# Attention heads issued in pairs over the two halves of the array, with the first mixer's masks added on VectorE

## Chip, core and metric

The kernel runs on one core of a Trainium2 chip. The metric is device time in microseconds for one execution. TensorE multiplies, VectorE and ScalarE work on tiles, SyncE issues the loads of weights. Each engine takes its instructions in the order of its own queue and waits on semaphores for the others.

## The reference

256 tokens of 1024 features go through two blocks. The parts that this change touches are the products of attention heads, all 64 wide:

```python
SEQ, D_MODEL, HEAD_DIM = 256, 1024, 64
ATTN_PATTERNS = ((128, 1), (512, 4), (2048, 16))     # window, dilation of three groups of four heads

def token_mixing(u, cos, sin, w_in, w_pool, pool_scale, w_pool_branch, w_attn_branch, w_out):
    p, q, k, v, gate_logits = jnp.split(u @ w_in, cuts, axis=-1)
    y_pool = multiscale_pool(p, w_pool, pool_scale)            # 4 groups of 64
    q, k = apply_rope(q, cos, sin), apply_rope(k, cos, sin)
    for gi, (window, dilation) in enumerate(ATTN_PATTERNS):
        o, lse = dilated_window_attention(q[:, :, hs], k[:, :, hs], v[:, :, hs], window // dilation, dilation)
    wts = jax.nn.softmax(jnp.stack(lses, axis=0), axis=0)      # joint over the three groups
    y_attn = jnp.einsum('gbsh,gbshd->bshd', wts, jnp.stack(outs, axis=0))
    gates = jax.nn.sigmoid(gate_logits)
    return (g_pool * (y_pool @ w_pool_branch) + g_attn * (y_attn @ w_attn_branch)) @ w_out

def second_block(x, ...):
    for l in range(2):
        ret_o = retention(rq, rk, r_v, r_g, ret_gn_w[l])                       # 4 heads, 64 wide
        swa_o = sliding_window_sink_attention(s_q, s_k, s_v, swa_sinks[l])     # 6 heads, 64 wide
        mla_o = latent_attention(...)                                          # 6 heads, keys of 96, values of 64
        mix = jnp.concatenate([ret_o, swa_o, mla_o], axis=-1) @ w_out[l]
        x = layer_norm(DEEPNORM_ALPHA * x + mix, ...)
        x = layer_norm(DEEPNORM_ALPHA * x + grouped_moe(x, ...), ...)
```

Block 1 is a feed-forward step, this `token_mixing`, and a second feed-forward step, each with its modulation.

## The kernel before

Activations lie transposed, features on partitions and the 256 tokens in the columns. Weights come from HBM as fp32 panels of 1 MB (`raw`, five buffers) and are split exactly into two parts: ScalarE casts the high one and VectorE subtracts it for the low one (both L254, 128x1024 a piece, into `hl`, six buffers). A product with a split weight is `mm3`, three matmuls (L249 to L251). Only the weights' products are split; the products inside attention are plain fp32, which TensorE runs in two pieces, so that a row of the trace counts each of them twice.

A scheduler sets the order on each engine when the program is built. It follows the program's dependences and its own model, and so it mixes a head's products with the split products of a projection. After that each queue is fixed.

The first mixer (`mixer`, L704) projects queries, keys and values, does the pooling branch (`dd`, L761 and L762: two products for each of four groups, two groups in the two column halves of a bank), and then runs a loop of four. An iteration takes the scores of one head in three groups (`scores`, L780 to L783), starts two gate panels, lets three panels of the modulation through (`drain`, each a pass of VectorE at L354 over 128x1024), takes the softmax (`softmax_rows`, L693 to L700), multiplies the gate panels (96 split products, `proj_t`), and then takes the head's values (`values`, L795 to L801). In a group the late 128 queries see 256 keys and the early ones 128. For each a matmul of an identity with the bf16 mask opens the PSUM region, and the 64-row product of queries and keys adds to it. For the values, three transposes go into one bank of the tag `x` (two buffers), `evac` copies 384 columns out as `pt` (two buffers; every third call of `evac` goes to VectorE at L687, the others to ScalarE at L685), and two 64-column products add into `y`.

Block 2 has two layers (`mixer2`). Heads come in pairs there: `pair_scores` (L981) puts the scores of two heads into one PSUM tile, one head after the other, `pair_softmax` normalises them and `pair_values` (L995) transposes, copies and multiplies head by head. The sliding-window pairs have 64 rows and a mask over both key blocks; the latent pairs have 96 rows and a mask over the diagonal block. The retention loop (L1204) takes a head's scores (`rs`, L1210 and L1211), multiplies them with the decay on VectorE (`sd`, L1213) and makes two products into `ry` (L1214, L1215). Other products of these layers are the latent projections, `uq` and `ukv` (L674 to L676), whose banks are copied out by `evac` as well.

PSUM has eight banks: two for `mm`, one each for `st` and `w` (where `y` and `ry` lie), two of the tag `x`, and the tile `s1` of two banks.

## Time and profile before

| | |
|---|---|
| runs | 1182.67, 1182.7, 1187.75 us |
| median of the runs | 1182.7 us |
| span of the profiled execution | 1186.2 us |
| TensorE busy | 1144.6 us, 96% |
| VectorE busy | 713.3 us, 60% |
| ScalarE busy | 511.4 us, 43% |
| DMA, share of 16 engines | 62.8%, 229 GB/s |
| mean granted clock of TensorE | 0.987 |

The profiled execution is one of its own, some 3.5 us longer than the median run. Spans on an engine are busy times of its instructions; a matmul's busy time reaches into the start of the next, so lengths of work on TensorE are best read from start to start.

### The profile page before, as it was taken

How to read it: one execution, taken by the hardware profiler on the slowest of the kernel's cores; microseconds unless marked ns; L12 is line 12 of the kernel's file. 1: busy time of each engine (PE TensorE's matmuls, PEld its weight loads, DVE VectorE, ACT ScalarE, POOL GpSimd, SP SyncE). 2: the span in 40 equal slices, each digit the busy share in tenths (PEclk: the TensorE clock that was granted, in tenths of full speed). 3: DMA queues.
4: the chain of work that ended last, by engine and by line, in shares of the span. 5: the costliest groups of instructions: out<-in, count | busy, mean ns of one | idle time of the engine just before them, and what ended most of it. 6: DMA issues, size and time to landing. Idle time of an engine off the chain costs nothing. (4 is left out here: it accounts for less than half of the span.)

```text
span 1186.2 us, 20785 instructions
## 1 busy us (share of the span) xinstructions
PE 1144.6 (96%) x8495; PEld 943.5 (80%) x8495; DVE 713.3 (60%) x1410; ACT 511.4 (43%) x946; POOL 44.5 (4%) x53
## 2 busy tenths in 40 slices
PE   6999999999999999999999998999989999899995
PEld 4999999988888999999997878544458787844443
DVE  5698879777877775555677754621258864451114
ACT  4454445534534554444556434222247643322213
POOL 0000001000000200000120001000001000100000
PEclk9999999999999999999999999999989999999998
DMA  9788779738863455535572439599743334779941
GB/s 317 292 362 307 288 258 325 263 133 316 306 230 112 173 180 182 184 125 183 168 250 99 143 109 353 216 385 390 290 155 135 136 109 170 288 272 397 380 156 38
DMA packets 77354, 272.12 MB, mean 229 GB/s; under 512 B 7873, under 2 KB 10817, under 8 KB 62914
## 3 DMA queue, kind: packets, MB, share of 16 engines
q1 hardware_dynamic: 77250, 270.70, 62.8%
q8 instruction: 70, 1.15, 0.4%
q14 instruction: 34, 0.28, 0.1%
HBM read 269.63 MB, written 1.05 MB: 228 GB/s over the span
## 5 line engine op out<-in xcount | busy, mean ns | idle before, releaser
L254 DVE TENSOR_TENSOR hl<-raw,hl 128x1024 fp32r<-128x1024 f32 (+5 forms) x267 | 293.4, 1108 | 120.8 <-ACT hl L254 120.0
L254 ACT CAST hl<-raw 128x1024 fp32r<-128x1024 f32 (+5 forms) x267 | 254.0, 958 | 233.9 <-PE mm L251 172.2
L249 PE MATMUL mm<-xh,hl 128*128 128x256 f32 x896 | 255.2, 286 | 4.0 <-ACT xh L254 3.3
L251 PE MATMUL mm<-xh,hl 128*128 128x256 f32 x896 | 255.2, 285 | 0.0
L250 PE MATMUL mm<-xl,hl 128*128 128x256 f32 x896 | 253.4, 283 | 0.0
L249 PEld LDWEIGHTS mm<-xh,hl 128*128 128x128 f32 x896 | 169.6, 190 | 6.6 <-ACT xh L254 3.6
L250 PEld LDWEIGHTS mm<-xl,hl 128*128 128x128 f32 x896 | 170.4, 190 | 1.9 <-issue 1.9
L251 PEld LDWEIGHTS mm<-xh,hl 128*128 128x128 f32 x896 | 170.4, 190 | 1.0 <-issue 1.0
L1632 PE MATMUL gu<-hl,xg 128*64 128x512 f32 x208 | 101.8, 604 | 0.0
L249 PE MATMUL mm<-gh,hl 128*128 128x256 f32 x352 | 99.2, 282 | 0.0
L251 PE MATMUL mm<-gh,hl 128*128 128x256 f32 x352 | 99.2, 282 | 0.0
L250 PE MATMUL mm<-gl,hl 128*128 128x256 f32 x352 | 99.2, 282 | 0.0
L1632 PE MATMUL gu<-raw,xg 128*64 128x512 f32 x192 | 92.9, 603 | 0.0
L354 DVE SCALAR_TENSOR_TENSOR raw<-raw,cond 128x1024 f32<-128x1024 f32 x64 | 76.7, 1219 | 10.0 <-DMA raw<-in_w_ada_dram 10.0
L1668 DVE SCALAR_TENSOR_TENSOR ysl<-dn,gsl,ysh 128x512 fp32r<-128x512 f32 x32 | 23.9, 750 | 75.8 <-ACT ysh L1667 75.8
L250 PEld LDWEIGHTS mm<-gl,hl 128*128 128x128 f32 x352 | 67.0, 190 | 0.0
L249 PEld LDWEIGHTS mm<-gh,hl 128*128 128x128 f32 x352 | 67.0, 190 | 0.0
L251 PEld LDWEIGHTS mm<-gh,hl 128*128 128x128 f32 x352 | 67.0, 190 | 0.0
L1632 PE MATMUL gu<-rawe,xg 128*64 128x512 f32 x112 | 54.6, 604 | 0.0
L1619 DVE TENSOR_SCALAR xg<-ga,cols 128x256 f32<-128x256 f32 x32 | 17.4, 543 | 55.8 <-ACT xg L1618 55.8
L1667 ACT ACTIVATE ysh<-dn,gsl 128x512 fp32r<-128x512 f32 x32 | 22.0, 687 | 55.7 <-PE dn L1665 55.7
L1618 ACT ACTIVATE xg<-ga,cols 128x256 f32<-128x256 f32 x32 | 18.1, 565 | 60.9 <-PE ga L1615 55.0
(531 smaller groups left out, 2428.3 us busy)
## 6 DMA issues: line engine op xcount, KB each, us to landing
raw<-in_w_ffn_in_dram SPq DMA_DIRECT2D x41, 1024.0 KB, 4.9
raw<-in_w_ada_dram SPq DMA_DIRECT2D x34, 1024.0 KB, 6.2
raw<-in_w_in_dram SPq DMA_DIRECT2D x34, 1024.0 KB, 5.0
hl<-in_gate_up_dram SPq DMA_DIRECT2D x26, 1024.0 KB, 8.5
raw<-in_gate_up_dram SPq DMA_DIRECT2D x24, 1024.0 KB, 7.9
raw<-in_w_ffn_out_dram SPq DMA_DIRECT2D x32, 704.0 KB, 4.2
rawe<-in_gate_up_dram SPq DMA_DIRECT2D x14, 1024.0 KB, 8.2
raw<-in_w_out_dram SPq DMA_DIRECT2D x12, 1024.0 KB, 4.9
```

The lines of the kernel that those rows point to most:

```text
L249: PE.matmul(o, wh, xh, start=first, stop=False)
L250: PE.matmul(o, wh, xl, start=False, stop=False)
L251: PE.matmul(o, wl, xh, start=False, stop=last)
L254: return S.copy(hi, x), V.tensor_tensor(out=lo, in0=x, in1=hi.bitcast(F32), op=ALU.subtract)
L354: V.scalar_tensor_tensor(out=w, in0=w, scalar=1.0, in1=cond, op0=ALU.mult, op1=ALU.mult, accum_out=mod[:, a + j:a + j + 1])
L1618: S.activation(out=xg[:, 2 * j], in_=p[:, :T], func=AF.Identity, scale=col(0, 2 * j), bias=col(8, 2 * j))
L1619: mark[0] = V.tensor_scalar(out=xg[:, 2 * j + 1], in0=p[:, T:], scalar1=col(0, 2 * j + 1), scalar2=col(8, 2 * j + 1), op0=ALU.mult, op1=AL ...
L1632: mm = PE.matmul(p[i * CAP:(i + 1) * CAP], xg[:, k, s], w[i][:, k % 4], start=(k == 0), stop=(k == KB - 1))
L1667: made = S.activation(out=ysh[:, c], in_=p, func=AF.Copy, scale=gc)
L1668: mark[0] = made, V.scalar_tensor_tensor(out=ysl[:, c], in0=p, scalar=gc, in1=ysh[:, c].bitcast(F32), op0=ALU.mult, op1=ALU.subtract)
```

## The change

In the first mixer the four heads become two pairs. The masks are no longer products: a pair's scores of a group go into one `s1` tile, a bank to each head, and VectorE adds the mask on the way into an SBUF tile `sb`. The softmax then works inside `sb`. The values of a pair take six transposes into one tile of the same tag `s1` (one buffer), one copy of 768 columns, and four products, the heads in turn. Scores and softmax of a pair stand a gate iteration ahead of the next pair's, and the values one and two iterations later.

```diff
+                def scores(j):
+                    sb = pool.tile([P, 2, 3, 3 * P], F32, name="sb", tag="sb", bufs=2)
                     for g in range(3):
-                        q, k = qT[r, g, h // 2], kT[r, g, h // 2]
-                        PE.matmul(s1[:, g], identb, mask[:, g * T:g * T + T], start=True, stop=False)
-                        PE.matmul(s1[:, g], q[:, P:], k, start=False, stop=True)
-                        PE.matmul(s0[:, g], identb, mask[:, g * T + P:g * T + T], start=True, stop=False)
-                        PE.matmul(s0[:, g], q[:, :P], k[:, :P], start=False, stop=True)
+                        s = pq.tile([P, 2, 2 * T], F32, name="s1", tag="s1", bufs=1)
+                        for i, r in enumerate(halves):
+                            PE.matmul(s[:, i, :T], qT[r, g, j, P:], kT[r, g, j], start=True, stop=True)
+                        for i, r in enumerate(halves):
+                            PE.matmul(s[:, i, T:T + P], qT[r, g, j, :P], kT[r, g, j, :P], start=True, stop=True)
+                        V.tensor_tensor(out=sb[:, :, g], in0=s[:, :, :3 * P], in1=mask[:, g:g + 1].to_broadcast([P, 2, 3 * P]), op=ALU.add)
...
+                def soft(sb):
+                    parts = [sb[:, :, :, :T], sb[:, :, :, T:]]
+                    for x in range(2):
+                        V.tensor_reduce(out=mx[:, 2 * x:2 * x + 2], in_=parts[x], op=ALU.max, axis=AX.XY)
+                    V.tensor_scalar(out=nb, in0=mx, scalar1=-0.125, scalar2=None, op0=ALU.mult)
+                    for p, c in every:
+                        S.activation(out=p, in_=p, func=AF.Exp, bias=nb[:, c], scale=0.125, accum_out=den[:, c])
+                    V.reciprocal(out=den, in_=den)
+                    for p, c in every:
+                        V.tensor_scalar(out=p, in0=p, scalar1=den[:, c], scalar2=None, op0=ALU.mult)
...
+                def values(j, sb):
                     y = bank("w", "y")
                     for g in range(3):
-                        tr = bank("x", "tr", pq)
...
-                        pt = pool.tile([P, 3 * P], F32, name="pt", tag="pt", bufs=2)
-                        evac(pt, tr[:, :3 * P])
-                        PE.matmul(y[r, :T], v[:, g, 0, c], pt[:, :T], start=(g == 0), stop=False)
-                        PE.matmul(y[r, P:T], v[:, g, 1, c], pt[:, T:], start=False, stop=(g == 2))
+                        tr = pq.tile([P, 2, 2 * T], F32, name="tr", tag="s1", bufs=1)
...
+                        pt = pool.tile([P, 2, 3 * P], F32, name="pt", tag="pt", bufs=1)
+                        evac(pt, tr[:, :, :3 * P])
+                        for t, o in enumerate((slice(0, T), slice(P, T))):
+                            for i, r in enumerate(halves):
+                                PE.matmul(y[r, o], v[:, g, t, (2 * j + i) * 64:(2 * j + i) * 64 + 64], pt[:, i, (0, T)[t]:(T, 3 * P)[t]],
+                                          start=(g + t == 0), stop=(g == 2 and t == 1))
...
+                sb = [scores(0)]
+                soft(sb[0])
+                gate(0)
+                sb.append(scores(1))
+                soft(sb[1])
+                gate(1)
+                values(0, sb[0])
+                gate(2)
+                values(1, sb[1])
+                gate(3)
```

`gate(i)` is the rest of the old loop's body. The pooling's products are issued group by group in turn instead of both of one group first. In block 2, the pairs of 64 rows get one mask product of 384 columns a head, and then the two late and the two early products in turn; the latent pairs stay as they were. `pair_values` and the retention go the same way as the first mixer's values: one tile of the tag `s1`, one pass of 768 columns, products in turn.

```diff
+            if q[0].shape[0] == 64:
+                for i in two:
+                    PE.matmul(s[:, 2 * i:2 * i + 2].rearrange("p a t -> p (a t)")[:, :3 * P], identb, mask, start=True, stop=False)
+                for i in two:
+                    PE.matmul(late[i], q[i][:, P:], k[i], start=False, stop=False)
+                for i in two:
+                    PE.matmul(early[i], q[i][:, :P], k[i][:, :P], start=False, stop=True)
...
-                        st = bank("x", "rs", pq)
...
-                        sd = pool.tile([P, 384], F32, name="sd", tag="pt", bufs=2)
-                        V.tensor_tensor(out=sd, in0=st[:, :384], in1=decay[:, 2 * b + i], op=ALU.mult)
...
+                    st = pq.tile([P, 2, 2 * T], F32, name="rs", tag="s1", bufs=1)
...
+                    sd = pool.tile([P, 2, 384], F32, name="sd", tag="pt", bufs=1)
+                    V.tensor_tensor(out=sd, in0=st[:, :, :384], in1=decay[:, 2 * b:2 * b + 2], op=ALU.mult)
```

Comments and docstrings are dropped too, so line numbers differ. The loads on SyncE and the work of GpSimd keep their order, and outside the mixers so does TensorE.

On TensorE in the first mixer, around a group's values: `tr` is the tile of transposes, `y` the values' products, `s` a head's scores (the numbers tell tiles apart). Before:

```order
L795 MATMUL tr<-k_c_mats,pr_3352 128x128
L796 MATMUL tr<-k_c_mats,pr_3361 128x128
L797 MATMUL tr<-k_c_mats,pr_3361 128x128
L780 LDWEIGHTS identb
L780 MATMUL s_3492<-mask,identb 128x256
L781 MATMUL s_3492<-kT,qT 128x256
L800 MATMUL y<-pt,v 64x256
L801 MATMUL y<-pt,v 64x128
L800 MATMUL y<-pt,v 64x256
L801 MATMUL y<-pt,v 64x128
L795 MATMUL tr<-k_c_mats,pr_3352 128x128
L796 MATMUL tr<-k_c_mats,pr_3361 128x128
```

After, with four more split products where the dots are:

```order
L802 MATMUL y<-pt,v 64x256 x2
L802 MATMUL y<-pt,v 64x128 x2
L797 MATMUL tr<-k_c_mats,sb 128x128 x6
L250 MATMUL mm<-xl,hl 128x256
L251 MATMUL mm<-xh,hl 128x256
L249 MATMUL mm<-xh,hl 128x256
...
L251 MATMUL mm<-xh,hl 128x256
L802 MATMUL y<-pt,v 64x256 x2
L802 MATMUL y<-pt,v 64x128 x2
L797 MATMUL tr<-k_c_mats,sb 128x128 x6
```

Before, the products of one head stood between transposes and scores of others; after, eight split products stand between a set of six transposes and the four products that need its copy.

On TensorE in block 2, layer 0, the scores of the third sliding-window pair. Before:

```order
L986 LDWEIGHTS identb
L986 MATMUL s_7218<-mask,identb 128x256
L987 MATMUL s_7218<-skT,sqT 128x256
L991 LDWEIGHTS identb
L991 MATMUL s_7218<-mask,identb 128x128
L992 MATMUL s_7218<-skT,sqT 128x128
L986 LDWEIGHTS identb
L986 MATMUL s_7218<-mask,identb 128x256
L987 MATMUL s_7218<-skT,sqT 128x256
L1000 MATMUL tr<-k_c_mats,pr 128x128
L1001 MATMUL tr<-k_c_mats,pr 128x128
L1002 MATMUL tr<-k_c_mats,pr 128x128
```

After, from the last transposes ahead of the second pair's values on:

```order
L676 MATMUL uq<-hl,cTh_7057 128x288
L1104 MATMUL tr<-k_c_mats,ckv 128x128 x2
L1023 MATMUL y<-pt,sv 64x256 x2
L1023 MATMUL y<-pt,sv 64x128 x2
L998 LDWEIGHTS identb
L998 MATMUL s_7126<-mask,identb 128x384
L998 LDWEIGHTS identb
L998 MATMUL s_7126<-mask,identb 128x384
L1000 MATMUL s_7126<-skT,sqT 128x256 x2
L1002 MATMUL s_7126<-skT,sqT 128x128 x2
L1104 MATMUL tr<-k_c_mats,ckv 128x128 x2
L674 MATMUL ukv<-hl,cTh_7209 128x384
```

The masks went ahead of all products, the two heads' products stand together, and the second pair's values (`y`) stand right ahead of them, where they stood behind.

On VectorE in the first mixer, at the start of the gate loop: `hl` are weight splits, L354 the modulation's panels, `ds` and `ypl` the pooling's. Before:

```order
L254 TENSOR_TENSOR hl<-raw,hl 128x1024 x2
L354 SCALAR_TENSOR_TENSOR raw,mods<-raw,cond 128x1024
L768 SCALAR_TENSOR_TENSOR ypl<-yp,k_pool_scale,yph 128x256
L687 COPY ds<-dd 128x256
L354 SCALAR_TENSOR_TENSOR raw,mods<-raw,cond 128x1024
L768 SCALAR_TENSOR_TENSOR ypl<-yp,k_pool_scale,yph 128x256
L693 TENSOR_REDUCE mx<-s_3303 128x1
L693 TENSOR_REDUCE mx<-s_3302 128x1
L695 TENSOR_SCALAR nb<-mx 128x1
L356 TENSOR_TENSOR mods<-mods,k_b_ada 128x2
L695 TENSOR_SCALAR nb<-mx 128x1
L354 SCALAR_TENSOR_TENSOR raw,mods<-raw,cond 128x1024
```

After:

```order
L254 TENSOR_TENSOR hl<-raw,hl 128x1024 x2
L773 TENSOR_TENSOR sb<-s_3304,mask 128x2x384
L756 SCALAR_TENSOR_TENSOR ypl<-yp,k_pool_scale,yph 128x256
L687 COPY ds<-dd 128x256
L354 SCALAR_TENSOR_TENSOR raw,mods<-raw,cond 128x1024 x2
L756 SCALAR_TENSOR_TENSOR ypl<-yp,k_pool_scale,yph 128x256
L773 TENSOR_TENSOR sb<-s_3310,mask 128x2x384
L356 TENSOR_TENSOR mods<-mods,k_b_ada 128x2
L354 SCALAR_TENSOR_TENSOR raw,mods<-raw,cond 128x1024
L254 TENSOR_TENSOR hl<-raw,hl 128x1024
L773 TENSOR_TENSOR sb<-s_3316,mask 128x2x384
L354 SCALAR_TENSOR_TENSOR raw,mods<-raw,cond 128x1024
```

The two reductions of the first head's scores are gone from here, and three additions `sb` stand among the splits and panels; the reductions follow after the third.

## Rows read from the trace of the kernel before

**Rows 1.** The page, parts 1 and 2: busy us, share, instructions; granted clock in 40 slices
```profile
PE 1144.6 (96%) x8495; PEld 943.5 (80%) x8495; DVE 713.3 (60%) x1410; ACT 511.4 (43%) x946; POOL 44.5 (4%) x53
PEclk9999999999999999999999999999989999999998
```

**Rows 2.** TensorE's waits: waiter, releaser, total us, times, longest
```profile
PE ukv L674 <- DVE vm L687: 1.6, 2, 0.8
```

**Rows 3.** Windows of the gate loop: busy us by engine, granted clock, DMA share, GB/s
```profile
285.60:305.00 19.40, 19.40 (x143) 16.19 (x142) 16.35 (x31) 9.76 (x16) 0.00 (x0) 1.00 0.88 326
305.00:324.00 19.00, 19.00 (x136) 16.17 (x135) 17.04 (x36) 7.73 (x14) 0.00 (x0) 1.00 0.81 307
324.00:343.00 19.00, 19.00 (x134) 15.79 (x133) 13.67 (x30) 7.47 (x14) 0.00 (x0) 1.00 0.65 229
343.00:360.00 17.00, 17.00 (x120) 14.09 (x119) 8.78 (x16) 7.50 (x13) 0.00 (x0) 1.00 0.50 200
```

**Rows 4.** Timeline of TensorE, one head's group: start, us, products (two pieces each in fp32)
```profile
327.55 0.28 PE L780 MATMUL s<-mask,identb 128*128 128x256 bf16 x1
327.76 0.70 PE L781 MATMUL s<-kT,qT 64*128 64x256 f32 x2
...
328.96 0.28 PE L780 MATMUL s<-mask,identb 128*128 128x256 bf16 x1
...
329.80 0.65 PE L800 MATMUL y<-pt,v 128*64 128x256 f32 x2
330.60 0.23 PE L782 MATMUL s<-mask,identb 128*128 128x128 bf16 x1
```

**Rows 5.** Windows, TensorE's products into y alone: layers 0 and 1 of block 2
```profile
600.00:760.00 160.00, 8.31 (x48) 0.99 0.51 182
860.00:1040.00 180.00, 8.79 (x48) 0.97 0.46 164
```

**Rows 6.** Timeline of TensorE: the pooling's products; a retention pair's scores
```profile
287.34 0.66 PE L761 MATMUL dd<-raw,pn 128*64 128x256 f32 x4
287.82 0.40 PE L762 MATMUL dd<-raw,pn 128*64 128x128 f32 x4
288.15 0.28 PE L780 MATMUL s<-mask,identb 128*128 128x256 bf16 x1
...
686.79 0.71 PE L1210 MATMUL rs<-rqT,rkT 64*128 64x256 f32 x4
687.33 0.40 PE L1211 MATMUL rs<-rqT,rkT 64*128 64x128 f32 x4
687.65 0.38 PE L249 MATMUL mm<-mixh,hl 128*128 128x256 f32 x1
687.88 0.28 PE L250 MATMUL mm<-mixl,hl 128*128 128x256 f32 x1
688.00 0.28 PE L251 MATMUL mm<-mixh,hl 128*128 128x256 f32 x1
```

**Rows 7.** Timeline of TensorE: a sliding-window pair's scores, first and following product
```profile
613.08 0.28 PE L986 MATMUL s<-mask,identb 128*128 128x256 bf16 x1
...
615.91 0.38 PE L1025 MATMUL mm<-hl,xh 128*128 128x256 f32 x1
```

**Rows 8.** Windows, the retention's products into ry alone: layer 0
```profile
600.00:760.00 160.00, 2.60 (x16) 0.99 0.51 182
```

**Rows 9.** VectorE by form (xcount, busy us, mean ns, idle before); the first two in 285:367
```profile
L254 DVE TENSOR_TENSOR hl<-raw,hl 128x1024 fp32r<-128x1024 f32 x18 | 22.0, 1221 | 6.7 <-ACT hl L254 6.7
L354 DVE SCALAR_TENSOR_TENSOR raw<-raw,cond 128x1024 f32<-128x1024 f32 x18 | 21.8, 1217 | 0.3 <-DMA raw<-in_w_ada_dram 0.3
...
L687 DVE COPY pt<-tr 128x384 f32<-128x384 f32 x14 | 7.8, 555 | 6.5 <-PE tr L797 3.6 <-PE tr L1002 2.9
L1213 DVE TENSOR_TENSOR sd<-rs,raw 128x384 f32<-128x384 f32 x8 | 4.3, 553 | 2.4 <-PE rs L1211 2.4
```

**Rows 10.** ScalarE by form, whole span: the copy of a head's transposed weights
```profile
L685 ACT COPY pt<-tr 128x384 f32<-128x384 f32 x22 | 10.1, 481 | 9.0 <-PE tr L1002 9.0
```

More of the change, by code (lines that the diff above doesn't have):

```diff
@@ L772, in mixer @@
                 yal = pool.tile([P, 2, T], F32R, name="yal")
-                def scores(h):
-                    r = slice(h % 2 * 64, h % 2 * 64 + 64)
-                    s1 = pq.tile([P, 4, T], F32, name="s1", tag="s1", bufs=1)
-                    s0 = bank("x", "s0", pq).rearrange("p (g k) -> p g k", g=4)
+                halves = [slice(i * 64, i * 64 + 64) for i in range(2)]
+                def scores(j):
+                    sb = pool.tile([P, 2, 3, 3 * P], F32, name="sb", tag="sb", bufs=2)
@@ L800, in values @@
-                        PE.matmul(y[r, :T], v[:, g, 0, c], pt[:, :T], start=(g == 0), stop=False)
-                        PE.matmul(y[r, P:T], v[:, g, 1, c], pt[:, T:], start=False, stop=(g == 2))
-                    split(yah[r, h // 2], yal[r, h // 2], y[r, :T])
+                        tr = pq.tile([P, 2, 2 * T], F32, name="tr", tag="s1", bufs=1)
+                        for i in range(2):
+                            for x, c in enumerate((slice(T, None), slice(0, P), slice(P, T))):
+                                PE.transpose(tr[:, i, x * P:(x + 1) * P], sb[:, i, g, c], ident)
@@ L804, in mixer, with gate @@
+                    split(yah[:, j], yal[:, j], y[:, :T])
                 tg = pool.tile([P, KB, 2 * T], F32, name="tg")
-                for i in range(4):
-                    s0, s1 = scores(i)
+                def gate(i):
                     wgp = weights(win[10 + i], KB, 256)
@@ L982, in pair_scores @@
             s = pq.tile([P, 4, T], F32, name="s1", tag="s1", bufs=1)
-            for i in range(2):
-                o, e = s[:, 2 * i], s[:, 2 * i + 1, :P]
-                if mask.shape[-1] == T:
-                    PE.matmul(o, identb, mask, start=True, stop=False)
-                    PE.matmul(o, q[i][:, P:], k[i], start=False, stop=True)
-                else:
-                    PE.matmul(o, q[i][:, P:], k[i], start=True, stop=False)
-                    PE.matmul(o[:, P:], identb, mask, start=False, stop=True)
-                PE.matmul(e, identb, mask[:, -P:], start=True, stop=False)
-                PE.matmul(e, q[i][:, :P], k[i][:, :P], start=False, stop=True)
+            two = range(2)
+            late, early = [s[:, 2 * i] for i in two], [s[:, 2 * i + 1, :P] for i in two]
+            if q[0].shape[0] == 64:
[5 more added lines that the diff above has]
+                    PE.matmul(early[i], q[i][:, :P], k[i][:, :P], start=False, stop=True)
+            else:
+                for i in two:
+                    PE.matmul(late[i], q[i][:, P:], k[i], start=True, stop=False)
+                    PE.matmul(late[i][:, P:], identb, mask[:, P:T], start=False, stop=True)
+                    PE.matmul(early[i], identb, mask[:, P:T], start=True, stop=False)
+                    PE.matmul(early[i], q[i][:, :P], k[i][:, :P], start=False, stop=True)
             return s
@@ L1045, in mixer2 @@
                 maskf = raw_tile(A["c_masks"].rearrange("p (a m) -> p a m", a=1), 1, 8 * P)[:, :8 * P]
-                mask = pool.tile([P, 2 * P], BF16, name="mask")
-                V.tensor_copy(mask, maskf[:, 6 * P:])
+                mask = pool.tile([P, 3 * P], BF16, name="mask")
+                V.tensor_copy(mask[:, :T], maskf[:, 6 * P:])
+                V.tensor_copy(mask[:, T:], maskf[:, 7 * P:])
                 sk = pool.tile([P, 3, 2, 2], F32, name="sk")
```

77 lines of the change are left out of this document (31 added, 46 removed).

## The prediction, made before the changed kernel ran

> **What bounds the kernel now.** I read the page's busy shares first, then TensorE's list of waits, then windows over the first mixer's attention, and only then single products. TensorE is busy 1144.6 of the 1186.2 us of the span, at the full clock (2.4 GHz, granted clock near 1.00) nearly throughout; VectorE is busy 60% [rows 1]. TensorE idles some 42 us in all. In the gate loop of the first mixer it is busy in every microsecond, VectorE for 16.35 of 19.40 us in the first stretch and 8.78 of 17 in the last, and the DMA share falls from 0.88 to 0.50 [rows 3]. So every product here is on the path: what is taken off TensorE is time saved, if no wait takes its place. The waits that exist are short; the one that resembles what the change adds (a product waiting for a bank that VectorE has yet to copy out) cost 0.8 us at the longest [rows 2].
>
> **Units.** A full 128x256 product of the split weights takes 0.12 us from start to start, and the first one after a plain fp32 product 0.23, so a switch costs 0.11 (687.65, 687.88, 688.00) [rows 6].
>
> **First mixer's scores.** One head and group now takes 1.41 us from its late mask to the next one's (327.55 to 328.96), of which the late mask product alone is 0.21 [rows 4]. There are 12, so 16.9 us. After, a pair of heads has two 256-key and two 128-key products on opposite row halves and no mask. The price of that set is already in the trace: the retention's products have the same shapes, and both heads of a pair ran in 0.86 us (686.79 to 687.65) [rows 6]. Six sets are 5.2 us: 11.7 saved.
>
> **First mixer's values.** The two 64-column products of a head alone take 0.80 us (329.80 to 330.60) [rows 4]; twelve of them are 9.6. The pooling's four products have the same shapes on the two column halves and ran in 0.81 us together (287.34 to 288.15) [rows 6]; six such sets are 4.9. The difference is 4.7; I take 4.5, since a few already stand next to another head's. The 36 transposes stay. The sets stand more often alone between split products, some six more switches at 0.11, 0.6 lost. First mixer: 11.7 + 4.5 - 0.6 = 15.6 us off TensorE.
>
> **Pooling.** Issued in turn now, but both halves overlapped already [rows 6]: nothing. Here the Trainium skill says otherwise. In "TensorE: Matmul & The Clock Gate", Part 3, it states that matmuls keep program order in start and end and are never reordered. By that, four products issued head by head would have run in two serial steps before, and the change would gain some 0.8 us here at each of two places and about as much at the retention, and the time would be 3 us lower than I say; the rows show both heads' first products ahead of either second one, so the trace disagrees and I count nothing.
>
> **Block 2 scores.** One pair of sliding-window heads takes 2.83 us (613.08 to 615.91) [rows 7]; two layers have three each. After: two 384-column mask products, at 0.21 each by the nearest row (the 256-column mask), and a row-half set at 0.86: 1.28. Six times 1.55 is 9.3 saved. The latent pairs have 96 rows and cannot pair: nothing.
>
> **Block 2 values.** 12 pairs held TensorE 8.31 + 8.79 = 17.1 us with tails [rows 5]. One set in turn is 0.88 with its tail (the pooling's, 287.34 to 287.82 and 0.40) [rows 6]: 12 x 0.88 = 10.6. Saved 6.5; some pairs overlap already, which is why it is not half.
>
> **Retention.** The value products of four pairs held 2.60 us in a layer, 1.30 a pair [rows 8]; in turn 0.88, four pairs save 1.7. The score products overlapped where nothing stood between them [rows 6]; for the others I take 0.8. Together 2.5.
>
> Off TensorE in all: 15.6 + 9.3 + 6.5 + 2.5 = **33.9 us**.
>
> **What the change adds.** Six mask additions of 128x768 on VectorE. A 384-wide product read from PSUM takes 553 ns there, a copy 555 [rows 9]; I take 0.95 us for 768. The softmax now reduces from SBUF the same number of elements, two reductions for a pair instead of four, so VectorE gains about 2 us of work against 18.6 us of idle time in the four stretches of the loop [rows 3]: no new bound. DMA and its order are untouched. The costs are hand-offs, because the scores tile and the tile of six transposes are now one PSUM tile with one buffer, and the copy out is one instruction of 768 where two of 384 took turns:
>
> - Scores of groups two and three wait until VectorE has added the mask of the group before. The additions stand in the queue behind two 1.22 us weight splits or modulation panels [rows 9]; queued behind the addition are the pooling's second subtraction, the panels and splits; TensorE stands meanwhile with all the gate products behind it. Walking the queues by the row durations gives 0.3 + 0.85 + 0.6 us for the three places where products ahead do not cover it, bounds 0 and 1.2 us (one split) for each of four.
> - Values: between a set of transposes and its products stand 8 split products at the shortest (0.95 us) and 12 at the longest. The copy of 768 takes 0.85 on ScalarE by twice 481 ns less the fixed part [rows 10], and 0.95 on VectorE plus its queue. Four on ScalarE wait 0.2 to 0.3, the two on VectorE 0.7 and 1.0 behind splits. Together with the scores about **5 us**, bounds 2 and 9.
> - Twelve copies out of PSUM become six, so whose turn it is (every third copy is VectorE's) shifts for all later ones; a 384-wide copy costs 481 or 555 ns by engine [rows 9, 10], so I take no net cost.
> - Block 2, a layer: six copies 0.3 us longer than before, with little cover (1.8); the retention's one multiplication of 768 instead of two of 384 (0.35); and two further waits like the one on a bank at 0.8 [rows 2], since the sliding-window scores and products now come earlier than ScalarE and VectorE deliver (1.6). About 3.75 a layer, **7.5 us**, bounds 3 and 13. Nearest row is the 0.8, so I stay near it.
>
> Net: 33.9 - 12.5 = 21.4 us. The profiled execution has a span of 1186.2, the runs a median of 1182.7; the work removed is the same in both. 1186.2 - 21.4 is 1164.8 for a profile, 1182.7 - 21.4 = 1161.3 for the median: **1161**. With waits between 5 and 22 us the forecast's own range is 1154 to 1171.
>
> **Rivals.**
> 1. *Hand-offs cost twice as much or a little more.* For it: one buffer where there were two, and additions in an in-order queue with 1.2 us pieces ahead. Against: VectorE is free for 16%, 10%, 28% and 48% of the loop's four stretches [rows 3], and the rows show no wait over 0.8 us on such a copy. Waits of 25 us instead of 12.5 leave 9: 1174. The Trainium skill, "TensorEngine Tiling (Array Packing)", section PSUM Bottleneck, says that tiling speeds up TensorE but not the copy out of PSUM, which may then be the bottleneck; that speaks for this rival, and the trace of before, with its double buffers, cannot settle it.
> 2. *Nearly all hidden.* The scheduler's products in between cover the hand-offs but for 2 us: 1151.
> 3. *Slower: the additions fall behind VectorE's queue.* If each of the eight VectorE hand-offs of the first mixer (six additions, two copies) meets two panels of 1.22 us and a split that itself waits for ScalarE (VectorE waited 6.7 us for ScalarE in this loop [rows 9]), 3.6 us each, that is 29 us over the forecast: 1190. It decides from 2.7 us each on. For it: the queue is in order and the addition stands behind exactly such pieces. Against: with a tenth to a half of each stretch idle on VectorE, the queue is seldom three deep.
> 4. *The halves do not overlap in the new order* and the change only drops masks: 12 x 0.21 of the late masks, the early ones at no more than that, so 4.4 with 0.16 for an early one, and 2 in block 2, against 12.5 of waits: 1189. Against: rows 6, the same shapes.
>
> **How the numbers follow.** Forecast 0.58, rival one 0.20, two 0.08, three 0.08, four 0.06. The predicted time is the forecast's. The range of 8 in 10: below 1150 lies a share of rival two, above 1176 rivals three and four and the tail of rival one; 1150 to 1176. A measurement of this kernel tells a difference from no change at about 0.5%, 5.9 us, so from 1177 to 1189. Faster by more holds the forecast, rival two and three quarters of rival one, 0.81; within it a quarter of rival one and a part of three and four, 0.10; slower 0.09.
>
> **What would show it.** In the profile after: the four 64-row products of a pair within about 0.86 us and the four 64-column ones within 0.81 where no wait stands ahead; TensorE's busy time about 30 us lower; its waits 10 to 15 us higher, on the mask addition, on the copies of 768 and, in block 2, on the latent product's bank; VectorE's busy time some 2 us changed, DMA unchanged. The gain should lie about 10 us in the first mixer and 11 us in the two mixers of block 2. I am wrong if single waits on the mask addition reach 2 us, if a half-array set takes 1.4 us or more, or if what is saved comes back as a wait for weights after the loop: the DMA share of 0.88 in the first stretch [rows 3] leaves little to hurry, and panels used up to 10 us earlier may not be there.

## The result, and the profile after

The changed kernel takes 1156.4 us (median of 1155.7 to 1161.73) against 1182.68 us, a ratio of 0.9766 (95% interval 0.9742 to 0.9791): 26.3 us less, where 21.4 were forecast. In a second set of runs the ratio was 0.9782 (0.9759 to 0.9805).

TensorE is still busy 96% of the span, with 34 us less work. The profile's page after has this line, which answers to [rows 1] (busy time, share, instructions):

```profile
PE 1110.8 (96%) x8459; PEld 925.6 (80%) x8459; DVE 715.0 (62%) x1391; ACT 507.9 (44%) x932; POOL 44.5 (4%) x53
```

VectorE gained 1.7 us and the DMA traffic is the same, 272.12 MB. The two profiled spans differ by 31.5 us, more than the medians: before's profiled execution had a start that was 4.2 us longer (221.0 us instead of 216.8 to the first product `la` of the mixer), in code that is the same in both. Its clock was at the low level there, from 28 us on; the window from 28 to 35 us (length, TensorE's busy time, granted clock, DMA share, GB/s), before and after:

```profile
28.00:35.00 7.00, 6.61 (x37) 0.51 1.05 403
...
28.00:35.00 7.00, 7.00 (x62) 1.00 1.05 404
```

This is an accident of the execution: over the 14 profiles of this document, the seven with such a stretch need 219.7 to 221.6 us to that product and the seven without it 216.5 to 217.4, and the changed kernel is in both groups. So I compare stages, cut at the same products in both programs, and not spans.

Four stages, as windows of TensorE: stretch, its length, TensorE's busy time (x instructions), granted clock, DMA share, GB/s. First the kernel before, in this order: the first mixer from its last rotation (`perm`) to the second feed-forward step's first product; layer 0 from its first product to the last router product; the entry of layer 1, from the last expert product to the first into `s`; and layer 1 from there.

```profile
263.85:403.00 139.15, 137.11 (x1031) 1.00 0.64 232
594.55:729.51 134.96, 132.76 (x988) 1.00 0.51 177
875.60:884.98 9.38, 4.58 (x43) 0.81 0.38 102
884.98:1021.88 136.90, 134.02 (x980) 0.99 0.47 167
```

The kernel after, the same four (behind TensorE's busy time stand four more: weight loads, VectorE, ScalarE and GpSimd):

```profile
259.62:383.25 123.63, 122.36 (x1007) 114.88 (x1006) 110.78 (x178) 63.06 (x97) 5.62 (x6) 1.00 0.71 261
574.78:704.14 129.36, 124.88 (x981) 111.93 (x980) 86.42 (x196) 61.84 (x146) 9.68 (x10) 0.99 0.52 185
850.20:862.63 12.43, 4.74 (x42) 3.10 (x41) 4.95 (x17) 5.75 (x16) 0.87 (x1) 0.74 0.51 157
862.63:992.11 129.48, 125.73 (x974) 113.32 (x973) 87.17 (x205) 65.90 (x157) 7.93 (x9) 0.97 0.47 170
```

The first mixer is 15.5 us shorter, the layers 5.6 and 7.4, and the entry of layer 1, whose work is the same, 3.1 us longer. In the first mixer TensorE's idle time (length less busy) did not grow but shrank, from 2.0 to 1.3 us.

Other executions of the changed kernel and of variants show how steady the stages are. The first mixer was 123.6 us in three of three profiles of the changed kernel and 139.2 in two of two of the kernel before. A layer at the full clock was 127.8 us, and 1.6 to 3.1 more where the granted clock fell (below).

The units came as forecast. TensorE's timeline after, a row set of the first mixer, a column set, and a sliding-window pair with its two masks ahead:

```profile
290.33 0.70 PE L770 MATMUL s<-kT,qT 64*128 64x256 f32 x4
290.86 0.39 PE L772 MATMUL s<-kT,qT 64*128 64x128 f32 x4
291.18 0.38 PE L250 MATMUL mm<-xl,hl 128*128 128x256 f32 x1
...
320.29 0.87 PE L802 MATMUL y<-pt,v 128*64 128x256 f32 x8
321.09 0.88 PE L797 MATMUL tr<-k_c_mats,sb 128*128 128x128 f32 x6
...
593.33 0.50 PE L998 MATMUL s<-mask,identb 128*128 128x384 bf16 x2
593.75 0.70 PE L1000 MATMUL s<-skT,sqT 64*128 64x256 f32 x4
594.29 0.39 PE L1002 MATMUL s<-skT,sqT 64*128 64x128 f32 x4
594.61 0.38 PE L1041 MATMUL mm<-hl,xh 128*128 128x256 f32 x1
```

Start to start these are 0.85, 0.80 and 1.28 us, against 2 x 1.41, 2 x 0.80 and 2.83 before [rows 4, 7]. VectorE and ScalarE by form have the prices of the long pieces, 950 to 955 ns and 796 ns, where 0.95 and 0.85 were taken:

```profile
L687 DVE COPY pt<-tr 128x768 f32<-128x768 f32 x8 | 7.6, 955 | 2.8 <-PE tr L1018 2.4 <-PE tr L797 0.4
L773 DVE TENSOR_TENSOR sb<-s,mask 128x768 f32<-128x768 f32 x6 | 5.7, 950 | 0.0
L685 ACT COPY pt<-tr 128x768 f32<-128x768 f32 x10 | 8.0, 796 | 3.7 <-PE tr L1018 1.9 <-PE tr L797 1.8
```

TensorE's waits after (waiter, releaser, total, times, longest), the main ones that are new or longer than before:

```profile
PE ukv L674 <- ACT vm L685: 3.5, 2, 1.7
PE la L251 <- issue: 2.9, 1, 2.9
PE rrb L1253 <- DVE r L1248: 2.6, 2, 1.3
PE tr L1104 <- DVE cq L1096: 1.3, 2, 1.0
PE uq L674 <- ACT qf L685: 0.6, 2, 0.3
PE s L770 <- DVE sb L773: 0.5, 1, 0.5
PE y L802 <- DVE pt L687: 0.2, 1, 0.2
```

None of the hand-offs that the prediction priced is large: 0.5 us for one mask addition and 0.2 for one copy in the first mixer. One wait is nearly gone there: the branch products waited 2.0 us for `e` before (three times) and 0.4 after. The last values now stand ahead of a whole gate iteration, which may be why; no run isolates it.

### The profile page after: what moved, and what is told of

It is laid out like the page before. It is cut to its first block, busy times and chain, and to the rows that moved or that the text cites. A ratio compares the mean times of both kernels' runs of the same rounds, so it can differ in the third digit from the quotient of the medians.

```text
span 1154.7 us, 20672 instructions
## 1 busy us (share of the span) xinstructions
PE 1110.8 (96%) x8459; PEld 925.6 (80%) x8459; DVE 715.0 (62%) x1391; ACT 507.9 (44%) x932; POOL 44.5 (4%) x53
## 2 busy tenths in 40 slices
DMA packets 77354, 272.12 MB, mean 236 GB/s; under 512 B 7873, under 2 KB 10817, under 8 KB 62914
## 5 line engine op out<-in xcount | busy, mean ns | idle before, releaser
L251 PE MATMUL mm<-xh,hl 128*128 128x256 f32 x896 | 254.4, 284 | 0.0
L250 PE MATMUL mm<-xl,hl 128*128 128x256 f32 x896 | 253.3, 283 | 0.0
L250 PEld LDWEIGHTS mm<-xl,hl 128*128 128x128 f32 x896 | 169.6, 189 | 1.8 <-issue 1.6
L251 PEld LDWEIGHTS mm<-xh,hl 128*128 128x128 f32 x896 | 169.6, 189 | 1.1 <-issue 1.0
L251 PE MATMUL mm<-gh,hl 128*128 128x256 f32 x352 | 99.2, 282 | 0.0
L250 PE MATMUL mm<-gl,hl 128*128 128x256 f32 x352 | 99.2, 282 | 0.0
L354 DVE SCALAR_TENSOR_TENSOR raw<-raw,cond 128x1024 f32<-128x1024 f32 x64 | 76.6, 1220 | 12.8 <-DMA raw<-in_w_ada_dram 12.8
L250 PEld LDWEIGHTS mm<-gl,hl 128*128 128x128 f32 x352 | 67.0, 190 | 0.0
L251 PEld LDWEIGHTS mm<-gh,hl 128*128 128x128 f32 x352 | 67.0, 190 | 0.0
```

The lines of the kernel that those rows point to most:

```text
L250: PE.matmul(o, wh, xl, start=False, stop=False)
L251: PE.matmul(o, wl, xh, start=False, stop=last)
L354: V.scalar_tensor_tensor(out=w, in0=w, scalar=1.0, in1=cond, op0=ALU.mult, op1=ALU.mult, accum_out=mod[:, a + j:a + j + 1])
```

## Experiments

My theory after the result: the gain is the overlap of two adjacent heads' products and the masks' absence; the hand-offs in the first mixer are hidden by split products that the scheduler puts between; the waits that were added in block 2 are on VectorE's and ScalarE's other work and not on the long copies. Its rivals are in the expectations. Each time stands beside that of the kernel before in the same set of runs. The untouched stages, the start and the entry of layer 1, differ by up to 5 us from one profile to another, and so the stage decides where the question is about 2 to 5 us. The stages, in us, one profile each:

| kernel | first mixer | layer 0 | entry of layer 1 | layer 1 | median of runs (before) |
|---|---|---|---|---|---|
| before | 139.2 | 135.0 | 9.4 | 136.9 | 1182.68 |
| before, again | 139.2 | 135.0 | 9.8 | 137.5 | 1188.44, one run (1186.22) |
| changed | 123.6 | 129.4 | 12.4 | 129.5 | 1156.4 (1182.68) |
| changed, again | 123.7 | 130.9 | 12.4 | 127.8 | 1160.97 (1185.1) |
| changed, third time | 123.7 | 127.8 | 12.5 | 128.4 | 1161.12, one run (1186.22) |
| first mixer only | 123.6 | 135.0 | 14.0 | 136.4 | 1175.05 (1186.4) |
| block 2 only | 139.2 | 127.7 | 10.0 | 128.0 | 1169.7 (1186.4) |
| head by head | 123.9 | 130.4 | 11.3 | 129.7 | 1160.1 (1186.4) |
| masks as products | 126.2 | 127.8 | 9.8 | 127.8 | 1157.3 (1186.4) |
| hand-offs doubled | 123.9 | 127.8 | 13.6 | 130.5 | 1159.12 (1185.1) |
| own banks | 127.5 | 129.9 | 13.3 | 131.0 | 1165.27 (1185.1) |
| latent copies on VectorE | 123.7 | 126.9 | 12.3 | 126.9 | 1152.87 (1185.1) |
| longer latent wait | 123.7 | 130.2 | 12.6 | 132.2 | 1161.6, one run (1186.22) |
| shifted | 123.7 | 126.9 | 9.7 | 127.5 | 1156.03 (1184.72) |

**The two halves of the change.** The first kernel has the new code in `mixer` alone, the second in block 2 alone.

> Only the first mixer's code is changed (pairs, masks on VectorE, pooling in turn); block 2 is that of before. Theory one: the first mixer's part is what the two profiles show between the start of its scores and the second feed-forward step, 15.6 us, since the split products that stand between hide nearly all hand-offs: 1167. Rival (the prediction's sum, 5 us of hand-offs in the first mixer): 10.6 us, 1172.

> Only block 2 is changed; the first mixer is that of before. Theory one: 5.6 to 5.8 us a layer, as the profiles show between the last weights' step of block 1 and the experts, some 11 us: 1171.5. The gains of the two halves should add up to the whole, 26.3 us. Rival (part of the first mixer's gain is a later wait that goes away, so that the halves do not add up): the two together differ from 26.3 by more than 3 us.

The first ran at a ratio of 0.9911 (0.9891 to 0.993), the second at 0.9863 (0.9839 to 0.9887). By the medians that is 11.4 and 16.7 us, which add up to 28.1, near the whole (26.3). Read by the totals alone, the first would have borne out the prediction's sum for the first mixer (10.6 us). Its stages say otherwise: the first mixer is 15.6 us shorter, and 4.6 us are lost in the entry of layer 1, which this kernel does not change (14.0 instead of 9.4; its cause is below). So theory one holds by stage. In the second kernel the layers gained 7.2 and 8.9 us, more than expected: the numbers expected came from layers with a lowered clock.

**In turn or head by head.** The edit at each place is of this kind:

```diff
                         for i, r in enumerate(halves):
                             PE.matmul(s[:, i, :T], qT[r, g, j, P:], kT[r, g, j], start=True, stop=True)
-                        for i, r in enumerate(halves):
                             PE.matmul(s[:, i, T:T + P], qT[r, g, j, :P], kT[r, g, j, :P], start=True, stop=True)
```

> The changed kernel, with each head's two products issued one after the other (late, early, then the next head) instead of in turn, at all places; tiles, masks and copies stay. Theory one, by the rows of the pooling and the retention in the kernel before: TensorE starts the second head's first product ahead of the first head's second one whichever was issued first, so nothing changes: 1156.4 within 2 us. Rival (products start in the order of issue, so that a pair in this order runs as two serial steps): 34 sets cost 0.4 to 0.6 us more each, 14 to 20 us: 1170 to 1176.

The first mixer is 0.3 us longer, and a set issued as late, early, late, early takes 0.86 us (294.18 to 295.04), as in turn:

```profile
294.18 0.71 PE L770 MATMUL s<-kT,qT 64*128 64x256 f32 x4
294.71 0.39 PE L771 MATMUL s<-kT,qT 64*128 64x128 f32 x4
295.04 0.38 PE L250 MATMUL mm<-xl,hl 128*128 128x256 f32 x1
```

Theory one holds for a set that stands alone: the order within it is worth next to nothing, and the total (1160.1 us, 3.7 over the 1156.4 expected, in a set where the kernel before was 3.7 longer too) is far from the rival's 14 to 20 us.

Who puts the second head's long product ahead, the scheduler or TensorE? This kernel's queue is not listed here, but a set that is torn apart tells. In the changed kernel the pooling's `dd` (282.27) stands between the two long products of the first set (281.52) and the two short ones (283.07). Here one short product stands ahead of `dd` as well:

```profile
285.07 0.71 PE L770 MATMUL s<-kT,qT 64*128 64x256 f32 x4
285.61 0.38 PE L771 MATMUL s<-kT,qT 64*128 64x128 f32 x2
285.92 0.88 PE L749 MATMUL dd<-raw,pn 128*64 128x256 f32 x8
286.73 0.48 PE L771 MATMUL s<-kT,qT 64*128 64x128 f32 x2
```

A queue in the order of the program (late, early, late, then `dd`, then early) is torn just so. Yet both long products started ahead of the short one that was issued between them. This speaks for TensorE, and against an order of the queue that holds between the two row halves; a list of the queue would settle it.

But theory one does not hold without exception. In the layers, TensorE's busy time is 125.9 and 126.0 us, some 1.3 to 2.6 more than in other kernels (one fall of the clock in layer 0 included), and the sets show where: at two places in a layer the scheduler tears a set apart. Here the first head's scores of a retention pair run alone, 0.84 us, and the second's follow at 959.29, after another product:

```profile
957.82 0.70 PE L1224 MATMUL rs<-rqT,rkT 64*128 64x256 f32 x2
958.35 0.38 PE L1225 MATMUL rs<-rqT,rkT 64*128 64x128 f32 x2
958.66 0.70 PE L1235 MATMUL rmu<-ro,k_c_mats 128*128 128x256 f32 x2
```

In turn, such a tear leaves both heads' long products together. The Trainium skill, "TensorE: Matmul & The Clock Gate", Part 3, states that matmuls keep program order in start and end. If the queue has the program's order, as the set at 285.07 suggests, this trace does not agree.

**Masks back on TensorE.** Six pairs' masks as two products of 384 columns, and a plain copy where VectorE added.

```diff
+                        for i in range(2):
+                            PE.matmul(s[:, i, :3 * P], identb, mask[:, g], start=True, stop=False)
...
-                        V.tensor_tensor(out=sb[:, :, g], in0=s[:, :, :3 * P], in1=mask[:, g:g + 1].to_broadcast([P, 2, 3 * P]), op=ALU.add)
+                        V.tensor_copy(sb[:, :, g], s[:, :, :3 * P])
```

> The changed kernel, but in the first mixer each pair's group has its two masks as products of 384 columns ahead of the heads' products, as in block 2, and VectorE copies the scores out without adding. Theory one: two mask products take 0.43 us on TensorE, six pairs of them 2.6, nothing else moves: 1159. Rival (the addition on VectorE is what the scores wait for): the copy is no cheaper than the addition, and the longer products cover part of the wait, so less than 1 us: 1157.

The first mixer is 2.5 us longer (126.2 instead of 123.6), as theory one had it, with 2.4 more of TensorE's busy time. So of the 15.5 us the masks on VectorE are 2.5. The rest, some 13, is the pairs and the merging of a head's two mask products into one, which this kernel has as well; the two are not told apart. The total (ratio 0.9758) does not show this, since this kernel escaped the loss at the entry of layer 1.

**Hand-offs doubled.** Every mask addition and every copy of 768 in the first mixer is done twice on the same engine.

```diff
                         V.tensor_tensor(out=sb[:, :, g], in0=s[:, :, :3 * P], in1=mask[:, g:g + 1].to_broadcast([P, 2, 3 * P]), op=ALU.add)
+                        V.tensor_tensor(out=sb[:, :, g], in0=s[:, :, :3 * P], in1=mask[:, g:g + 1].to_broadcast([P, 2, 3 * P]), op=ALU.add)
...
                         evac(pt, tr[:, :, :3 * P])
+                        evac_i[0] -= 1
+                        evac(pt, tr[:, :, :3 * P])
```

> The changed kernel with each mask addition and each copy of 768 columns in the first mixer done twice, on the same engine, with the same result; block 2 is untouched. Theory one (hand-offs are hidden because the 8 to 12 split products between just cover one copy): the six copies have no cover left, 0.85 to 0.95 each, and two of the four additions that are waited for, so the stage is 6 to 7 us longer: 15.6 saved becomes 9. Rival A (ample cover): under 2 us longer. Rival B (VectorE's queue is full, as the prediction's third rival had it): over 12 us longer.

The first mixer is 0.3 us longer: rival A, and my account of why was wrong. The cover is not a fixed 8 to 12 split products. With the longer piece in the program, the scheduler puts more products in between at five of six places. In the changed kernel 40, 8, 12, 8, 8 and 11 split products stand between a set of transposes and its values; here it is 21, 42, 32, 15, 15 and 20. (The 40, the first set's, is beyond the 12 that the prediction gave as the longest.) The timeline around one copy, without the split products:

```profile
318.69 0.87 PE L798 MATMUL tr<-k_c_mats,sb 128*128 128x128 f32 x6
...
324.74 0.76 PE L805 MATMUL y<-pt,v 128*64 128x256 f32 x6
```

There are 384 gate products in the loop to take from, so a hand-off twice as long costs next to nothing. It also takes away the prediction's first and third rivals, as far as the first mixer goes.

**A bank to each head.** The transposes of each head go to a bank of their own, copied at the same time by the two engines, 384 columns each.

```diff
+                        for i in range(2):
+                            tr = bank("x", "tr", pq)
...
+                            (S.copy, V.tensor_copy)[i](pt[:, i], tr[:, :3 * P])
```

> The changed kernel, but each head's three transposes go into a bank of their own (two buffers, as in the kernel before), and are copied as 384 columns, the first head's by ScalarE and the second's by VectorE at the same time; the products stay in turn. Theory one (copies of 768 are already covered): every stage within 1 us of the changed kernel. Rival (the single tile and its one long copy cost what the prediction took for them, some 3 us in the first mixer and 1.8 a layer): 4 to 6 us faster in all.

Neither theory came out: the kernel is slower, 1165.27 us beside 1160.97 of the changed kernel in the same set. The first mixer takes 3.8 us more, all of it busy time, and the layers' busy time is 127.3 and 128.8 us, against 123.3 and 124.0 to 124.7 in other kernels at the full clock.

```profile
259.55:387.01 127.46, 126.03 (x1007) 1.00 0.70 254
...
578.58:708.46 129.88, 127.28 (x982) 1.00 0.51 180
868.19:999.15 130.96, 128.81 (x973) 0.99 0.46 162
```

The timeline shows why. The first head's product (315.94) is ready ahead of the second's, the scheduler lets it go, transposes and split products follow, and the rest comes at 317.71:

```profile
315.94 0.65 PE L802 MATMUL y<-pt,v 128*64 128x256 f32 x2
316.52 0.55 PE L798 MATMUL tr<-k_c_mats,sb 128*128 128x128 f32 x3
...
317.71 0.86 PE L802 MATMUL y<-pt,v 128*64 128x256 f32 x6
318.51 0.33 PE L798 MATMUL tr<-k_c_mats,sb 128*128 128x128 f32 x1
```

The first product alone takes 0.58 us and the rest 0.80, against 0.80 for all four together. Five of the six sets of the first mixer are torn in this way, some 2.9 of the 3.8 us. So what pairs the heads is that one tile and one copy make both ready at once. The long copy that the prediction counted as a cost is what holds the pair together.

**The wait for the latent banks.**

```diff
-                        evac(kf[:, t, 3 * n:3 * n + 3, :64], pv[:, :, :64])
-                        evac(vm[:, t, 3 * n:3 * n + 3], pv[:, :, 64:])
+                        copy = S.copy if t else V.tensor_copy
+                        copy(kf[:, t, 3 * n:3 * n + 3, :64], pv[:, :, :64])
+                        copy(vm[:, t, 3 * n:3 * n + 3], pv[:, :, 64:])
+                        evac_i[0] += 2
```

> The changed kernel, but the first two banks of the latent keys and values (ukv) are copied out by VectorE and the last two by ScalarE, whatever the turn. Theory one (the product waits 1.7 us a layer because the copy stands on ScalarE behind the four exponentials of the third pair): the wait falls to 0.5 or less, each layer 1.2 us shorter, and more where the clock fell behind it: 1.2 to 2.7 a layer. Rival (the wait is for something that VectorE has as late, such as the reductions of the same pair): layers unchanged within 0.5 us, the wait named on VectorE.

Theory one holds. In the changed kernel the copies of the bank stand on ScalarE behind the exponentials (L980), and the product `ukv` behind them:

```profile
623.75 0.37 ACT L980 ACTIVATE pr<-s,nb 128x128 f32<-128x128 f32 x1
...
624.39 0.57 ACT L685 COPY vm<-ukv 128x192 f32<-128x192 f32 x2
...
624.79 0.44 PE L674 MATMUL ukv<-hl,cTh 128*128 128x384 f32 x1 [1.72 <-ACT vm L685]
```

With the copies on VectorE the wait fell to 0.5 us:

```profile
PE ukv L674 <- DVE vm L1154: 0.9, 2, 0.5
```

Both layers are 126.9 us without a fall of the clock, 0.9 less than 127.8, where 1.2 was expected. The whole takes 1152.87 us (ratio 0.9728, 0.9705 to 0.975), less than both kernels; that is 8 us below the changed kernel of the same set, of which some 3 is the start in the two profiles (217.1 and 220.2 us) and not the copies.

**The same kernels again, and a longer wait.** To see what belongs to the change: the kernel before and the changed one once more, and one in which three of the latent copies are repeated twice more on ScalarE.

> The kernel before, profiled a second time. The stages that the change touches repeat: 139.2 us from the first mixer's last rotation to the second feed-forward step, 134.9 us in layer 0 and 134.9 to 136.9 in layer 1. The start (217 or 221 us to the first mixer) and the entry of layer 1 (9.4 to 14 us over all traces so far) are the same code in all kernels. Theory one: they vary by chance, and a second trace shows another value than 221.0 and 9.4 at one of them. Rival: the entry is longer because of the change, and stays at 9.4 to 10 in the kernel before.

> The changed kernel again, beside the others of this set. By stage the traces so far give 15.6 us in the first mixer, 5.6 to 7.2 in layer 0 and 7.6 to 9.2 in layer 1, where the lower ends are executions in which TensorE's granted clock fell to about 0.55 for some 2 us behind a wait. Theory one: those stages again, ratio 0.975 to 0.977. Rival (the layers' gains differ by chance of the loads, not by the clock): a layer at 5.6 without a stretch of low clock.

> The changed kernel, profiled a third time: 123.6 us in the first mixer, each layer 127.8 at the full clock, and 1.5 to 3 more where the granted clock falls behind a wait; the entry of layer 1 between 9.8 and 14 (theory one) or again near 12.4 (rival: it belongs to the change).

> The changed kernel, with the copies of three of the latent banks (vm of ukv) done three times on ScalarE, so that the product behind waits longer: 1.7 us becomes 2.5 to 3 by the row of one such copy (0.32). Theory one (the clock falls by chance behind waits of this length): each layer 127.8 + 1 to 2 of wait, and a stretch of granted clock near 0.55 behind it, more often than behind 1.7. Rival (the falls have nothing to do with these waits): the clock stays at 1.00 in both layers.

The stages that the change touches repeat, and the layers that gained least (130.9 and 129.4 us) are ones in which the clock fell; the ratio of the second set, 0.9782, lies a little above the 0.975 to 0.977 expected. The entry of layer 1 is 9.4 and 9.8 us in the kernel before and 12.4, 12.4 and 12.5 in the changed one: theory one (chance) is wrong, the 2.9 us belong to the program. The start does vary by chance, 216.5 to 221.6 us over all kernels, with the clock at 28 us.

In the layers, the clock: in the changed kernel layers without a fall take 127.8 us (128.4 in one layer 1 that begins 1.3 us longer at the low clock), with one 129.4 to 129.5, with two 130.5 to 130.9 (the higher in the changed kernel, the lower in the one with doubled hand-offs), so a fall costs 1.4 to 1.6 us. Layer 1 begins at the low clock in every kernel, and that is not counted here. Behind the 1.7 us wait for the latent bank it fell in 4 of the 14 layers with that wait that were profiled, behind 2.6 us (the longer wait) in both, and behind 0.5 us in none of four. Behind the retention's 1.3 us wait (`rrb`) it fell in 4 of 20. The granted clock behind the wait, in layer 1 of the changed kernel (first profile), in layer 1 of the one with the longer wait, and in layer 0 of the one with only block 2 changed, which has the same 1.7 us and no fall:

```profile
914.00:916.00 2.00, 2.00 (x11) 0.52 0.72 274
...
916.00:918.00 2.00, 2.00 (x10) 0.50 0.90 381
...
642.00:644.00 2.00, 2.00 (x17) 1.00 0.76 279
```

What decides whether the clock falls at one and the same wait stays open; that a longer wait makes the fall likelier rests on few layers.

**The entry of layer 1.** In the changed kernel it holds a gap in the middle of a product, and what ends it is named "issue": TensorE waited for nothing but its instructions.

```profile
857.89 0.58 PE L249 MATMUL la<-xh,hl 128*128 128x258 f32 x1 [4.77 <-DMA s<-in_sinks_dram]
...
858.98 0.56 PE L250 MATMUL la<-xl,hl 128*128 128x258 f32 x1
862.46 0.38 PE L251 MATMUL la<-xh,hl 128*128 128x258 f32 x1 [2.92 <-issue]
```

A 16 KB load of the instruction queue starts at 860.1, while the layer's first weights come in, and is over 1.4 us ahead of 862.46. If the place at which such a piece ends makes the gap, then the gap should stand at one count of instructions, whatever stands there. The traces bear this out. Counted over all of TensorE's records, weight loads and waits included, the instruction that comes late is the 13,193rd in all nine profiles with a gap: `la` L251 in the changed kernel, `la` L250 with the latent copies on VectorE, a product into `ss` with doubled hand-offs. In the kernel with the first mixer only it is one of TensorE's semaphore instructions, inside the long wait of the entry (863.5 to 868.1), which is why that entry takes 14.0 us. In the five profiles without a gap the 13,193rd record stands ahead of that wait or at its start.

By the same reading, some instructions more ahead of the entry move the gap away. The last kernel adds 12 products that nothing reads to the router's wait, on top of the latent copies on VectorE.

```diff
                 with tc.issue_after(summed.ins):
-                    busy(20)
+                    busy(32)
```

> The kernel with the latent copies on VectorE first (e8), and 12 more of the products that nothing reads in the router's wait of each layer (3 us of TensorE idle), which puts 24 more instructions of TensorE ahead of layer 1. In the three traces of the changed kernel and in that of e8, the entry of layer 1 holds a gap of 2.5 to 2.9 us at the second or third product, which waits for nothing but instructions and ends 1.4 us behind a 16 KB load of the instruction queue; the kernel with mask products has 24 instructions more ahead of it and no gap. Theory one (the place at which the loaded piece of the instruction stream ends makes the gap): entry 9.4 to 10 us instead of 12.3, the whole 2.5 us faster than e8, 1150.4. Rival (the gap belongs to the earlier arrival, which meets a load of weights): 12.3 again, 1152.9.

The entry is 9.7 us, against 12.3 without these products, and the gap is gone, as theory one had it. The total is not the 1150.4 expected and not better than that of the kernel with the latent copies on VectorE (1156.03 us on another set, ratio 0.9736): the added products did not stay free, and the stage from the router's last product to the first expert product went from 15.5 and 17.0 us in the two layers to 18.4 in both.

## Why the prediction was right, and where it was not

- *What bounds the kernel.* Right. Work taken off TensorE came out of the time, with VectorE and DMA where they were.
- *Off TensorE.* First mixer 15.6 forecast, 14.75 measured as busy time (137.11 to 122.36). A layer of block 2: 9.15 forecast, 9.5 measured where the clock did not fall (132.76 to 123.27). The unit prices taken from the pooling and the retention [rows 6] held to 0.01 us; they were for the same shapes. (The "four pairs" that held 2.60 us in a layer are two a layer; the sum counts them rightly.)
- *Hand-offs in the first mixer.* This is the term that was mis-sized: 5 us forecast, the idle time fell by 0.8. The walk through the queues took the products between as fixed, 8 to 12, and the 1.22 us pieces ahead as exposed. Doubling every piece cost 0.3 us, with more products in between at most places; and 1.6 us of the wait for `e` went away, which the prediction did not see. Its sign that TensorE's waits would be 10 to 15 us higher did not come: TensorE's idle time in the whole span went from 41.6 to 43.9 us.
- *Hand-offs in block 2.* 3.75 a layer forecast, 2.3 measured (idle 2.20 before, 4.47 with only block 2 changed). The size was near, the parts were not: the copies of 768, 1.8 us of the forecast, show no wait to speak of. The waits on banks, forecast at 1.6 by the row of 0.8 [rows 2], are there: the latent bank 1.7 in place of 0.8, the transposes of the latent query 1.0 (0.3 in layer 1), `uq` 0.3, and the retention's `rrb` 1.3 in place of 1.0. For the latent bank the cause is shown: its copy stood behind the exponentials on ScalarE, and moving copies to VectorE removed most of the wait. Before, the wait was for a copy on VectorE [rows 2]. So the shift of `evac`'s turns, which the prediction took at no net cost, can matter through the queue in which a copy then stands; how much of the 1.7 us is the turn and how much the earlier product is open. That the other waits come from TensorE's earlier arrival is argued, not shown.
- *What was not in the sum.* A fall of the clock (1.6 us each, in some executions) and 2.9 us at the entry of layer 1. They took back about what the hand-offs of the first mixer did not cost, so the total came as near as it did partly by luck. In the profile shown first the four stages give 15.5 + 5.6 + 7.4 - 3.1 = 25.4 us; measured were 26.3.
- *The rivals.* The halves overlap (rival four is out), VectorE's queue has room (three is out), doubled hand-offs are free in the first mixer (one is out there). Nearly all hidden (two) is what the first mixer did. The page that spoke for rival one, the Trainium skill's "TensorEngine Tiling (Array Packing)", section PSUM Bottleneck, says that copies out of PSUM may become the bottleneck once TensorE is faster; in this kernel's traces they did not.
- *The "in turn" of the change* brought little by itself, as the prediction said of the pooling: 0.3 us over the whole first mixer, and 1 to 2 us a layer where sets are torn apart.

## What to carry to other kernels

In these traces two half-array products overlap when they stand next to each other, nearly whichever is issued first; what matters is that nothing of full width comes between, and the surest way is one tile and one copy for both, so that they become ready together. Before a longer hand-off is priced as a wait, ask whether the scheduler has other products to put in between: where it has, even a doubled hand-off can be nearly free, and where the program has little else (here the latent part of block 2), look at which engine's queue the next copy stands in. And compare by stages that are cut at the same products: a total that is 4 us off can hide the whole effect of a part.

## What the runs showed of the hardware that I had not expected

- TensorE's clock fell from 2.4 to 1.2 GHz (granted share 0.50 to 0.52 in the stretches above) behind idle times of 1.3 to 2.6 us in the middle of busy work (4 of 20 layers at 1.3, 4 of 14 at 1.7, 2 of 2 at 2.6), in some executions and not in others of the same program; each fall cost 1.4 to 1.6 us on top of the wait. With one from 28 us on, the start of the changed kernel was 3.4 and 4.8 us longer than without.
- Two products of different heads on the two row halves started together at 285.07, ahead of a short product that the program has between them; whether that is the queue's order is inferred from a torn set, not listed.
- A gap of 2.5 to 2.9 us in which TensorE waited only for instructions, at the same product in three of three profiles of one program (1.8 to 4.5 us in other kernels), and at the 13,193rd record in all nine profiles that have one; it was gone when 24 instructions more stood ahead of it. That the end of a loaded piece of the instruction stream makes it is inferred from the load's time, the count and this shift; its size was not taken apart.
